# An eight-core decoder block: the order of the first transfers, and tile 0 scaled while the shift rows arrive

## The chip, the cores and the metric

The kernel runs on all 8 cores of one Trainium2 chip. Each core does one sequence of the batch and streams all the weights for itself; nothing is exchanged between cores. The metric is device time in microseconds (us) of the slowest core. An execution counts as slow, and is left out of every comparison, when one die is over 1% longer than the other at a lower granted TensorE clock, or when the run is over 1.5% above the fastest of the same kernel.

## The reference, cut to what matters

The block is a half-step SwiGLU feed-forward (FFN), a token mixer and a second FFN. Each is fed by an RMS norm whose scale and shift come from a conditioning vector:

```python
def ada_rmsnorm(x, g, shift, scale):
    return rmsnorm(x, g) * (1.0 + scale[:, None, :]) + shift[:, None, :]

def reference(x, c, w_mod, b_mod, g_ffn1, w_ffn1_in, w_ffn1_out, ...):
    c_act = jax.nn.silu(c)                                  # (8, 1024)
    mod = c_act @ w_mod[l] + b_mod[l]                       # (8, 9 * 1024)
    sh1, sc1, gt1, sh2, sc2, gt2, sh3, sc3, gt3 = jnp.split(mod, 9, axis=-1)
    h = ada_rmsnorm(x, g_ffn1[l], sh1, sc1)                 # x: (8, 4096, 1024) float32
    x = x + 0.5 * gt1[:, None, :] * swiglu_ffn(h, w_ffn1_in[l], w_ffn1_out[l])
    # ... mixer with sh2, sc2, gt2; second FFN with sh3, sc3, gt3; final norm
```

So nothing of the first FFN can be multiplied before 8 + 8 blocks of `w_mod` (those of `sc1` and `sh1`, 512 KB each) have been read. A core needs that much only once, at the very start.

Of the kernel before, what the change touches and what calls it, by code (L numbers as in the profile page):

```python
# [335 lines left out]
def build_program(n_tiles=SEQ // T, verbose=False):  # L336
# [17 lines left out]
    with es:  # L354
# [103 lines left out]

        def load_slab(nm, r, cast, prio=None, after=()):
            b = new(sl, f"{nm}{r}")  # L460
            if cast:
                src = dr(w_src[nm], r)
                dma("PL", lambda: b.ap, lambda: src, D_CAST, slot_sem(b, "PL"), [], [b], slab=True, prio=prio, after=after)
                d = scr[nm][r]
                dma("SP", lambda: d.ap, lambda: b.ap, D_SLAB, lambda: wb_sems[b.slot], [b], [d], prio=prio)
            else:
                d = scr[nm][r]
                dma("SP", lambda: b.ap, lambda: d.ap, D_SLAB, slot_sem(b), [d], [b], slab=True, prio=prio, after=after)
            return b
# [4 lines left out]
        dma("SP", lambda: crow.ap, lambda: crow_d[:, :], D_SLAB, lambda: sem_c, [], [crow], prio=-30)  # L474
        dma("PL", lambda: gates.ap, lambda: gates_d[:, :].rearrange("p (c n) -> p c n", c=8), 1.0, lambda: sem_g, [], [gates], prio=5000, after=(None,))
        sem_v, sem_c, sem_g = newsem("s_vecs"), newsem("s_crow"), newsem("s_gates")
# [11 lines left out]
        def mods(m, afters):  # L488

            for q in range(8):  # L490
                b = new(sl, f"mod{m + q}")
                src = dr(wmod_d, m + q)
                dma("SP", lambda b=b: b.ap.bitcast(F32), lambda s=src: s, D_SLAB, slot_sem(b), [], [b], slab=True,
                    prio=P.prio)
                o = modr[m].ap[:, q:q + 1]

                def f(b=b, o=o):
                    w = b.ap.bitcast(F32)
                    return lambda h: [h.scalar_tensor_tensor(out=w, in0=w, scalar=1.0, in1=crow.ap, op0=ALU.mult,  # L499
                                                             op1=ALU.mult, accum_out=o)]  # L500
                A("DVE", 1.3, f, [crow], [b, modr[m]], after=(afters[q],))
            tt(k_(modv[m].ap), k_(modr[m].ap), k_(V[:, V_BMOD + m:V_BMOD + m + 8]), ALU.add, [modr[m], vecs], [modv[m]], dur=0.17)

        def gs_op(m, g):
# [8 lines left out]
        P.prio = -20  # L513
        mods(M_SH1, [None] * 8)
        P.prio = 4000
# [42 lines left out]

        def ffn_in(slab, hbs, hids, j):

            w = lambda kc, o: (lambda: slab.ap[:, kc * 256 + o:kc * 256 + o + 128])
            ops = []
            for hb, hid in zip(hbs, hids):
                bg = new(ps, "g")
                mms(bg, [(w(kc, 0), lambda kc=kc, hb=hb: hb[kc].ap) for kc in range(8)], [slab] + hb)
                bu = new(ps, "u")
# [38 lines left out]
        for pi, tiles in enumerate(pairs):  # L605
            P.prio = 500 + pi * 100
            lp = -25 if pi == 0 else 400 + pi * 100
            xss = [load_x(x_dr, t, prio=(-22 if t == 0 else -15) if pi == 0 else lp, after=prev_in[8 * (t % 2):8 * (t % 2) + 8]) for t in tiles]
            hbs = [norm(xs, M_SC1, M_SH1, after=(last_in,), prio=300) for xs in xss]
            hids = [[] for _ in tiles]  # L610
            next_in = []
            for j in range(FC):
                slab = load_slab("w1i", j, pi == 0)
                ops = ffn_in(slab, hbs, hids, j)
                anchors.append((pi, ops[-1]))
# [19 lines left out]
        if len(pairs) == 1:  # L635
            mid = [mid[0]]

        psem = [VB(ap=None) for _ in range(8)]
# [179 lines left out]
        for s, op in seq:  # L818
            if op.nbytes == 0:
                for b in op.reads + op.writes:  # L820
                    if b.pool is sl and b not in use:
                        use[b] = len(use)
        loads.sort(key=lambda o: use[o.writes[0]])
        order = {o: k for k, o in enumerate(loads)}
# [142 lines left out]
```

## The kernel before: the parts that the change touches

A core's 4096 tokens are 8 tiles of 512. The first FFN takes the tiles in pairs: tiles 0 and 1, then 2 and 3, and so on. The weights are float32 in HBM, the chip's main memory. In the first pair each weight slab is loaded by a casting DMA to bf16 on GpSimd's queue and then written back as bf16 from SyncE's queue, so that later pairs can load it plainly.

The program is a list of operations. A planner simulates it once, picks by `prio` (low goes first) among those that are ready, and so fixes the order on each engine. Three kinds of relation matter here. A read or write of a buffer, and `sync`, become semaphore waits on the chip. `after` moves an operation only in the planned order; on the chip nothing waits for it. Every engine's list is written in the planned order, and ready work behind a wait was seen to stay behind it: in the changed kernel VectorE stood 4.3 us before two rows of `w_mod` while the scalings planned behind them were ready.

```python
def load_slab(nm, r, cast, prio=None, after=()):
    b = new(sl, f"{nm}{r}")                     # one of 10 slab buffers
    if cast:
        src = dr(w_src[nm], r)
        dma("PL", ..., D_CAST, slot_sem(b, "PL"), [], [b], slab=True, prio=prio, after=after)
        d = scr[nm][r]
        dma("SP", lambda: d.ap, lambda: b.ap, D_SLAB, lambda: wb_sems[b.slot], [b], [d], prio=prio)  # write-back
    else:
        dma("SP", ..., D_SLAB, slot_sem(b), [d], [b], slab=True, prio=prio, after=after)
    return b

def mods(m, afters):                            # one vector of `mod`: 8 rows of w_mod
    for q in range(8):
        b = new(sl, f"mod{m + q}")
        dma("SP", ..., D_SLAB, slot_sem(b), [], [b], slab=True, prio=P.prio)
        # VectorE: row * c_act, summed into modr[m][:, q]
        A("DVE", 1.3, f, [crow], [b, modr[m]], after=(afters[q],))
    tt(modv[m], modr[m], b_mod, ADD)            # all 8 sums, plus the bias

P.prio = -24
mods(M_SC1, [None] * 8)                         # scale rows
gs_op(M_SC1, V_G1)
P.prio = -20
mods(M_SH1, [None] * 8)                         # shift rows

def norm(xs, msc, msh, after=(), prio=None):
    r = stats(xs, after, prio)                  # 8 squares, 8 matmuls with ones, Ln, Exp
    for f in range(8):
        stt(t_, xs[f], gs[msc][f], r, MULT, MULT)        # VectorE: the scaling
        act(hb[f], t_, Identity, bias=modv[msh][f])      # ScalarE or VectorE: the shift

for pi, tiles in enumerate(pairs):
    lp = -25 if pi == 0 else 400 + pi * 100
    xss = [load_x(x_dr, t, prio=(-22 if t == 0 else -15) if pi == 0 else lp,
                  after=prev_in[8 * (t % 2):8 * (t % 2) + 8]) for t in tiles]
    hbs = [norm(xs, M_SC1, M_SH1, after=(last_in,), prio=300) for xs in xss]
    for j in range(FC):                         # 22 slabs of the first matrix
        slab = load_slab("w1i", j, pi == 0)
        ops = ffn_in(slab, hbs, hids, j)        # per tile: 8 gate and 8 up matmuls
        if j >= 3:
            next_in.append(ops[-1])
    prev_in = next_in
    if pi == 0:
        mods(M_GT1, [gt_anchor] * 8)            # gate rows
    for q in range(4):                          # 12 slabs of the second matrix
        slabs = [load_slab("w1o", 3 * q + s, pi == 0) for s in range(3)]
        ops = ffn_out(slabs, q, xss, hids, gth[M_GT1])
# ...
loads.sort(key=lambda o: use[o.writes[0]])      # slab buffers are given out in the order of first use
```

The norm of the next pair needs its x before the second matrix of this pair is done: in TensorE's order the eight statistics matmuls of tiles 2 and 3 stand within the work of the first pair.

## Time and profile before

| | before |
|---|---|
| time, median of 3 runs | 2489.81 us (2488.01 to 2493.35) |
| span of the profiled execution, slowest core | 2483.8 us |
| TensorE busy | 95% |
| first weight matmul | 65.82 us |
| TensorE reaches the statistics of tiles 2 and 3 | 220.50 us |
| TensorE goes on with weight matmuls | 235.36 us |

The page of the profile of before, its line of busy times and the chain of work that ended last (PE is TensorE, PEld its weight loads, DVE VectorE, ACT ScalarE, POOL GpSimd, SPq SyncE's issuing of transfers):

```profile
PE 2361.1 (95%) x11177; PEld 1114.5 (45%) x11392; DVE 1057.8 (43%) x1795; ACT 911.9 (37%) x1382; POOL 115.2 (5%) x221
...
PE 90%; DMA 5%; ACT 2%; issue 1%; SPq 1%; DVE 1%; POOL 0%; DVEq 0%; POOLq 0%; ACTq 0%
PE ps L443 90%; DMA sb_slab<-wmod 2%; DMA sb_c<-x 1%; SPq L450 1%; DMA sb_c<-xmid 1%; ACT sb_c L401 1%; DMA sb_slab<-w2o 1%; ACT sb_h L401 1%; DVE sb_c L419 0%; DVE sb_c L409 0%; DVE sb_slab L499 0%; DVE sb_ub L419 0%; ACT L401 0%; POOL y L450 0%; DVEq L113 0%
```

The kernel is bound by TensorE (PE). What the change can win is in the 5% that the chain spends on DMA: the rows of `wmod` and the tiles of x.

TensorE's timeline of before shows where that is. Columns: start, duration, engine, source line, operation, output and inputs, shapes, count, and in brackets the idle time before the group and what ended it. `sb_ones` are statistics, `sb_slab` are weight matmuls. Every matmul has one line of the program, so one goes by the inputs:

```profile
65.82 154.84 PE L443 MATMUL ps<-sb_h,sb_slab 128*128 128x512 bf16 x690 [15.81 <-ACT sb_h L401]
220.50 0.38 PE L443 MATMUL ps<-sb_h,sb_ones 128*128 128x512 bf16 x1
...
232.06 0.59 PE L443 MATMUL ps<-sb_h,sb_ones 128*128 128x512 bf16 x1 [5.14 <-ACT sb_h L401]
232.44 2.77 PE L443 MATMUL ps<-sb_h,sb_slab 128*128 128x512 bf16 x6
235.10 0.42 PE L443 MATMUL ps<-sb_h,sb_ones 128*128 128x512 bf16 x1
235.36 26.93 PE L443 MATMUL ps<-sb_h,sb_slab 128*128 128x512 bf16 x122
```

Three numbers will serve as marks: the **first weight matmul** (65.82), the **arrival** at the statistics of tiles 2 and 3 (220.50), and the **resume** of weight matmuls after them (235.36). The **stretch** between arrival and resume is 14.9 us here. At the next such change nothing is waited for and it takes 8.2 us (arrival 458.5, resume 466.73).

The same profile by windows. Columns: window, its length, busy time and count of PE, PEld, DVE, ACT and POOL, granted TensorE clock, mean busy share of the 16 DMA engines, GB/s:

```profile
12.00:28.00 16.00, 4.62 (x8) 0.84 (x8) 7.32 (x13) 7.62 (x11) 0.00 (x0) 1.00 0.99 325
34.00:46.00 12.00, 1.76 (x3) 0.31 (x3) 0.00 (x0) 1.92 (x4) 0.00 (x0) 1.00 1.02 199
72.00:86.00 14.00, 13.95 (x65) 6.37 (x65) 6.02 (x9) 3.61 (x6) 1.06 (x2) 1.00 0.38 119
86.00:100.00 14.00, 13.89 (x64) 6.37 (x65) 9.20 (x19) 2.39 (x4) 4.22 (x8) 1.00 0.88 149
```

DMA is full from 10 to about 70 us (a share of 0.97 to 1.02 by windows of 10 us), is then 38% busy for 14 us, and full again from 100 us (1.03 from 100 to 130 us). At 34 to 46 us it moves only 199 GB/s though it is full (1.02). The view of the DMA queues of that window says why: q0 carries the weight casts, q1 everything that SyncE issues.

```profile
q0 software_dynamic: 394, 1.43, 72.5%
q1 hardware_dynamic: 522, 0.95, 28.8%
```

The columns are packets, MB and share of the 16 engines. A cast packet holds an engine for 353 ns (72.5% of 12 us on 16 engines, over 394), a plain one for 106 ns; the cast packets are also larger here, 3.6 KB against 1.8 KB in the mean. So with both queues full in this window, plain loads got little more than a quarter of the time (28.8%).

### The profile page before, as it was taken

To read this page: it belongs to the slowest core of one execution; us is meant where nothing else is said; L and a number is where in the kernel's file an instruction comes from. 1 tells how busy PE (TensorE), PEld (TensorE's weight loads), DVE (VectorE), ACT (ScalarE), POOL (GpSimd) and SP (SyncE) were. 2 spreads that over 40 slices of the span, in tenths; PEclk is the share of its full clock that TensorE was granted. 3 is DMA by queue.
4 is the path that set the end of the run, shared out by engine and by line. 5 is a ranking of instruction groups with operands and counts; after the bars stand their busy time and mean duration, and the time that the engine had idled before them with its cause. 6 is when DMAs were issued, how large, how long until landed. Compare 5 with 4: busy or idle time off the path is not lost.

```text
span 2483.8 us, 34258 instructions; the slowest of 8 cores (2468.5 to 2483.8 us)
## 1 busy us (share of the span) xinstructions
PE 2361.1 (95%) x11177; PEld 1114.5 (45%) x11392; DVE 1057.8 (43%) x1795; ACT 911.9 (37%) x1382; POOL 115.2 (5%) x221
## 2 busy tenths in 40 slices
PE   1999999999999999899899999999999999999996
PEld 0444444444444444454354454454454454454442
DVE  3413133423342332785166175184274274373121
ACT  3213011301131120676157265265364364364122
POOL 0100100010001001000000000000000000000000
PEclk9999999999999999899999999999999999999998
DMA  9899489669856764554966555555555545555451
GB/s 274 192 217 230 160 213 221 165 189 220 221 166 181 188 189 164 163 166 159 200 207 203 186 179 178 187 178 179 187 178 178 187 170 187 187 170 186 153 188 66
DMA packets 131708, 460.31 MB, mean 185 GB/s; under 512 B 16048, under 2 KB 16176, under 8 KB 130864
## 3 DMA queue, kind: packets, MB, share of 16 engines
q1 hardware_dynamic: 113184, 378.15, 47.0%
q0 software_dynamic: 18352, 79.97, 16.0%
q8 instruction: 96, 1.57, 0.3%
q14 instruction: 76, 0.62, 0.1%
HBM read 446.78 MB, written 79.69 MB: 212 GB/s over the span
## 4 chain that ended last, share of the span: by engine, by line
PE 90%; DMA 5%; ACT 2%; issue 1%; SPq 1%; DVE 1%; POOL 0%; DVEq 0%; POOLq 0%; ACTq 0%
PE ps L443 90%; DMA sb_slab<-wmod 2%; DMA sb_c<-x 1%; SPq L450 1%; DMA sb_c<-xmid 1%; ACT sb_c L401 1%; DMA sb_slab<-w2o 1%; ACT sb_h L401 1%; DVE sb_c L419 0%; DVE sb_c L409 0%; DVE sb_slab L499 0%; DVE sb_ub L419 0%; ACT L401 0%; POOL y L450 0%; DVEq L113 0%
## 5 line engine op out<-in xcount | busy, mean ns | idle before, releaser
L443 PE MATMUL ps<-sb_h,sb_slab 128*128 128x512 bf16 x9776 | 2182.2, 380 | 28.7 <-ACT sb_h L401 15.8
L443 PEld LDWEIGHTS ps<-sb_h,sb_slab 128*128 128x128 bf16 x9984 | 977.7, 98 | 1196.1 <-issue 30.4
L423 DVE TENSOR_TENSOR sb_h<-ps,sb_c 128x512 bf16<-128x512 f32 x352 | 241.7, 691 | 784.0 <-PE ps L443 706.5
L401 ACT ACTIVATE sb_c<-ps 128x512 f32<-128x512 f32 x400 | 237.2, 596 | 882.0 <-PE ps L443 858.5
L401 ACT ACTIVATE sb_h<-sb_c 128x512 bf16<-128x512 f32 x241 | 148.9, 628 | 387.2 <-DVE sb_c L419 234.4
L419 DVE SCALAR_TENSOR_TENSOR sb_c<-ps,sb_gth,sb_c 128x512 f32<-128x512 f32 x128 | 95.2, 749 | 399.1 <-PE ps L443 390.6
L401 ACT ACT_TABLE_LOAD x102 | 130.9, 1283 | 211.5 <-PE ps L443 199.2
L419 DVE SCALAR_TENSOR_TENSOR sb_c<-sb_c,sb_gs 128x512 f32<-128x512 f32 x256 | 173.6, 745 | 39.9 <-ACT sb_c L401 39.9
L443 PE MATMUL ps<-sb_h,sb_ones 128*128 128x512 bf16 x313 | 106.6, 394 | 67.0 <-ACT sb_h L401 59.6
L499 DVE SCALAR_TENSOR_TENSOR sb_slab<-sb_slab,sb_crow 128x1024 f32<-128x1024 f32 x88 | 107.0, 1217 | 34.1 <-DMA sb_slab<-wmod 33.6
L443 PE MATMUL ps<-sb_ub,sb_slab 128*128 128x256 bf16 x1024 | 115.0, 273 | 4.3 <-DVE sb_c L409 3.3
L401 ACT ACTIVATE sb_h<-sb_c,sb_modv 128x512 bf16<-128x512 f32 x162 | 107.4, 719 | 15.6 <-DVE sb_modv L423 8.8
L443 PEld LDWEIGHTS ps<-sb_ub,sb_slab 128*128 128x128 bf16 x1024 | 99.5, 98 | 21.5 <-issue 8.1
L450 POOL DMA_DIRECT2D y<-sb_c x64 | 34.5, 540 | 1144.6 <-ACT sb_c L401 1104.7
L443 PEld LDWEIGHTS ps<-sb_h,sb_ones 128*128 128x128 bf16 x320 | 31.2, 98 | 118.5 <-issue 92.6
L419 DVE SCALAR_TENSOR_TENSOR sb_c<-ps,sb_modv,sb_c 128x512 f32<-128x512 f32 x64 | 48.0, 750 | 72.7 <-PE ps L443 72.5
L419 DVE SCALAR_TENSOR_TENSOR sb_c<-sb_ux,sb_vecs,sb_c 128x512 f32<-128x512 f32 x96 | 69.2, 743 | 1.3
L423 DVE TENSOR_TENSOR sb_c<-sb_c 128x512 f32<-128x512 f32 x96 | 61.6, 683 | 11.1 <-ACT sb_c L401 11.0
L419 DVE SCALAR_TENSOR_TENSOR sb_ub<-sb_c,ps 64x256 bf16<-64x256 f32 x128 | 53.8, 420 | 15.3 <-PE ps L443 11.8
L401 ACT ACTIVATE sb_c<-sb_c,sb_lam 128x512 f32<-128x512 f32 x64 | 49.1, 824 | 0.2
L450 POOL DMA_DIRECT2D xmid<-sb_c x64 | 34.8, 544 | 295.6 <-DVE sb_c L419 280.6
L401 ACT ACTIVATE sb_c<-sb_c 128x512 f32<-128x512 f32 x72 | 44.0, 626 | 2.2
(51 smaller groups left out, 532.8 us busy)
## 6 DMA issues: line engine op xcount, KB each, us to landing
sb_slab<-b_w2i SPq DMA_DIRECT2D x176, 512.0 KB, 3.8
sb_slab<-wmod SPq DMA_DIRECT2D x88, 512.0 KB, 6.1
sb_slab<-b_w2o SPq DMA_DIRECT2D x84, 512.0 KB, 3.7
sb_slab<-b_w1i SPq DMA_DIRECT2D x66, 512.0 KB, 6.0
sb_slab<-b_win SPq DMA_DIRECT2D x64, 512.0 KB, 4.0
sb_slab<-b_dcw SPq DMA_DIRECT2D x64, 512.0 KB, 3.6
sb_slab<-b_w1o SPq DMA_DIRECT2D x36, 512.0 KB, 5.5
sb_c<-x SPq DMA_DIRECT2D x64, 256.0 KB, 11.0
```

The source lines that it names most:

```text
L401: return A("ACT", dur, lambda: (lambda o, i: (lambda h: [h.activation(out=o, in_=i, func=func, bias=bias, scale=scale)]))(out(), in_()), r ...
L419: return A("DVE", dur, lambda: (lambda o, a, b: (lambda h: [h.scalar_tensor_tensor(out=o, in0=a, scalar=scalar, in1=b, op0=op0, op1=op1)]) ...
L423: return A("DVE", dur, lambda: (lambda o, a, b: (lambda h: [h.tensor_tensor(out=o, in0=a, in1=b, op=op)]))(out(), in0(), in1()), reads, wr ...
L443: return [h.matmul(o, lhsT=l, rhs=r, start=(first and i == 0), stop=(last and i == n - 1)) for i, (l, r) in enumerate(pr)]
L450: lambda: (lambda o, i: (lambda h: [h.dma_start(out=o, in_=i)]))(out(), in_()),
L499: return lambda h: [h.scalar_tensor_tensor(out=w, in0=w, scalar=1.0, in1=crow.ap, op0=ALU.mult, op1=ALU.mult, accum_out=o)]
```

## The change

The intent: the first transfers go in the order in which they are needed. Scale rows, x of tile 0, shift rows, then x of tile 1 and the third and later weight casts. Tile 0 is scaled while the shift rows are still arriving, and the first slab's gate matmuls for each block of the norm may start when that block is ready.

Its parts: (A) slab buffers are given out by priority before order of use, so that the 16 rows go ahead of weight casts; (B) x of tile 1 is planned after the last shift row; (C) casts from the third slab on wait at run time for the last shift row's multiplication, and are planned after x of tile 1; (D) the norm of tile 0 gets a high priority; (E) the first slab's gate matmuls are split into eight operations that wait separately; (F) the load of the mixer's gate weights moves to a later point.

```diff
-        def load_slab(nm, r, cast, prio=None, after=()):
+        def load_slab(nm, r, cast, prio=None, after=(), sync=()):
 ...
-                dma("PL", ..., D_CAST, slot_sem(b, "PL"), [], [b], slab=True, prio=prio, after=after)
+                dma("PL", ..., D_CAST, slot_sem(b, "PL"), [], [b], slab=True, prio=prio, after=after, sync=sync)
 ...
-        dma("PL", lambda: gates.ap, ..., [], [gates], prio=5000, after=(None,))
 ...
-        mods(M_SH1, [None] * 8)
+        sh1_last = mods(M_SH1, [None] * 8)
 ...
+                if split:
+                    for kc in range(8):
+                        mms(bg, [(w(kc, 0), ...hb[kc].ap)], [slab, hb[kc]], first=(kc == 0), last=(kc == 7))
+                else:
+                    mms(bg, [... for kc in range(8)], [slab] + hb)
 ...
-            xss = [load_x(x_dr, t, prio=(-22 if t == 0 else -15) if pi == 0 else lp, after=prev_in[8 * (t % 2):8 * (t % 2) + 8]) for t in tiles]
-            hbs = [norm(xs, M_SC1, M_SH1, after=(last_in,), prio=300) for xs in xss]
+            if pi == 0:
+                xss = [load_x(x_dr, t, prio=-22 if t == 0 else -15, after=[None if t == 0 else sh1_last] * 8) for t in tiles]
+                hbs = [norm(xs, M_SC1, M_SH1, prio=-23 if t == 0 else 300) for t, xs in zip(tiles, xss)]
+            else:
+                (as before)
 ...
-                slab = load_slab("w1i", j, pi == 0)
-                ops = ffn_in(slab, hbs, hids, j)
+                slab = load_slab("w1i", j, pi == 0, sync=(sh1_last,) if pi == 0 and j >= 2 else (),
+                                 after=[xb.lw for xb in xss[-1]] if pi == 0 and j >= 2 else ())
+                ops = ffn_in(slab, hbs, hids, j, split=(j == 0))
 ...
+        dma("PL", lambda: gates.ap, ..., [], [gates], prio=5000, sync=(mid[0],))
 ...
-        loads.sort(key=lambda o: use[o.writes[0]])
+        loads.sort(key=lambda o: (min(o.prio, 0), use[o.writes[0]]))
```

More of the change, by code (lines that the diff above doesn't have):

```diff
@@ L462, in load_slab @@
                 src = dr(w_src[nm], r)
-                dma("PL", lambda: b.ap, lambda: src, D_CAST, slot_sem(b, "PL"), [], [b], slab=True, prio=prio, after=after)
+                dma("PL", lambda: b.ap, lambda: src, D_CAST, slot_sem(b, "PL"), [], [b], slab=True, prio=prio, after=after, sync=sync)
                 d = scr[nm][r]
@@ L474, in build_program @@
         dma("SP", lambda: crow.ap, lambda: crow_d[:, :], D_SLAB, lambda: sem_c, [], [crow], prio=-30)
-        dma("PL", lambda: gates.ap, lambda: gates_d[:, :].rearrange("p (c n) -> p c n", c=8), 1.0, lambda: sem_g, [], [gates], prio=5000, after=(None,))
         sem_v, sem_c, sem_g = newsem("s_vecs"), newsem("s_crow"), newsem("s_gates")
@@ L500, in f @@
                                                              op1=ALU.mult, accum_out=o)]
-                A("DVE", 1.3, f, [crow], [b, modr[m]], after=(afters[q],))
+                last = A("DVE", 1.3, f, [crow], [b, modr[m]], after=(afters[q],))
             tt(k_(modv[m].ap), k_(modr[m].ap), k_(V[:, V_BMOD + m:V_BMOD + m + 8]), ALU.add, [modr[m], vecs], [modv[m]], dur=0.17)
+            return last
         def gs_op(m, g):
@@ L557, in norm, with ffn_in @@
             return hb
-        def ffn_in(slab, hbs, hids, j):
+        def ffn_in(slab, hbs, hids, j, split=False):
             w = lambda kc, o: (lambda: slab.ap[:, kc * 256 + o:kc * 256 + o + 128])
@@ L564, in ffn_in @@
                 bg = new(ps, "g")
-                mms(bg, [(w(kc, 0), lambda kc=kc, hb=hb: hb[kc].ap) for kc in range(8)], [slab] + hb)
+                if split:
+                    for kc in range(8):
+                        mms(bg, [(w(kc, 0), lambda kc=kc, hb=hb: hb[kc].ap)], [slab, hb[kc]], first=(kc == 0), last=(kc == 7))
+                else:
+                    mms(bg, [(w(kc, 0), lambda kc=kc, hb=hb: hb[kc].ap) for kc in range(8)], [slab] + hb)
                 bu = new(ps, "u")
@@ L607, in build_program @@
             lp = -25 if pi == 0 else 400 + pi * 100
-            xss = [load_x(x_dr, t, prio=(-22 if t == 0 else -15) if pi == 0 else lp, after=prev_in[8 * (t % 2):8 * (t % 2) + 8]) for t in tiles]
-            hbs = [norm(xs, M_SC1, M_SH1, after=(last_in,), prio=300) for xs in xss]
+            if pi == 0:
+                xss = [load_x(x_dr, t, prio=-22 if t == 0 else -15, after=[None if t == 0 else sh1_last] * 8) for t in tiles]
+                hbs = [norm(xs, M_SC1, M_SH1, prio=-23 if t == 0 else 300) for t, xs in zip(tiles, xss)]
+            else:
+                xss = [load_x(x_dr, t, prio=lp, after=prev_in[8 * (t % 2):8 * (t % 2) + 8]) for t in tiles]
+                hbs = [norm(xs, M_SC1, M_SH1, after=(last_in,), prio=300) for xs in xss]
             hids = [[] for _ in tiles]
@@ L636, in build_program @@
             mid = [mid[0]]
+        dma("PL", lambda: gates.ap, lambda: gates_d[:, :].rearrange("p (c n) -> p c n", c=8), 1.0, lambda: sem_g, [], [gates], prio=5000, sync=(mid[0],))
         psem = [VB(ap=None) for _ in range(8)]
```

## The prediction

> **What bounds the kernel now.** TensorE. Busy 95% of the 2483.8 us span; the chain of waits is 90% matmul. The change touches only the start and what follows from it. Timeline: real matmuls start at 65.82 us. In those 65 us the limit is DMA (share 0.97 to 1.02 per 10 us window from 10 to 70). The chain there is mostly scale/shift row loads (pieces of 14.9 and 23.3 us); the last of 16 rows is multiplied at 58-59 us, although tile 1 of x (landed 32 to 48 us) and three weight casts went ahead of them. A second cost falls at the change to tiles 2 and 3: the last x tiles land at 231 and 234 us, and the statistics stretch from 220.5 to 235.4 us takes 14.9 us against 8.2 us at the next such change (458.5 to 466.7). Between 72 and 86 us the DMA share is only about 37%, from 86 to 96 about 83%: some 10 us unused.
>
> **What changes.** Only the first stage's order differs; no work is removed. Ahead of the first weight matmul go vectors, 16 rows, x tile 0 (11.1 MB) and two casts; x tile 1, the third cast, six gate rows and the gate weights move behind. Estimate: 11.1 MB at the 325 GB/s of 12-28 us is 34 us, two casts at 3.2 us (23% of 42 us for three), a slow first 10 us: rows landed about 45-46 us, first weight matmul about 48.5 us (17 us earlier).
>
> Not all is won. TensorE is in order, and after 14 weight matmuls stand the statistics of tile 1. Its x queues behind the shift rows and one write-back. When the last shift row is multiplied, eight casts are released at once. [...]from 34 to 46 us, beside casts, the hardware queue moved 522 packets, 0.95 MB (79 GB/s) against 394 cast packets taking 72.5% of the time. I estimate four x tiles through before the casts bite, the other four at 79 GB/s: last x of tile 1 at 60-64 us, then about 5.6 us (square, statistics, table load 1.28, Ln, Exp, scale, shift). So 48 weight matmuls are done at about 77.5 us against 79.1 before: only 1 to 3 us won here.
>
> The rest comes later: eight casts in flight fill the idle DMA of 72-96 us, so next x should land about 222-226 us and most of the 8 us lost at 220-235 goes.
>
> **Prediction.** 2482 us (8 less), range 2473 to 2491. Faster by over 2% 0.01, same 0.98, slower 0.01.
>
> **What would show it.** First weight matmul 46-51 us; then TensorE idle for over 8 us waiting on squares of tile 1; x of tile 1 landing at intervals of 3 us or more once casts start; DMA share above 0.8 through 70-96 us; statistics stretch of tiles 2 and 3 down from 14.9 us to 8-11 us.
>
> **What would make it wrong.** If x of tile 1 slips past the casts (landed by 53 us), the start wins 10 us or more, and the gain is 12-18 us. If casts starve it to beyond 70 us, the start loses and the total is level. If SyncE blocks on its in-order waits (a gate row waits until TensorE has finished weight slab 4), next x comes no earlier and the switch gives nothing back.

The 79 GB/s and the 72.5% are measured (before, 34 to 46 us). The sum is as it stands: 34 us for 11.1 MB, 6.4 us for two casts and the slow first 10 us (a DMA share of 0.71, 163 GB/s in before) give rows at 45 to 46 us; of the 17 us won at the first weight matmul 1 to 3 us are kept, and with the stretch 4 to 7 us shorter (8 to 11 instead of 14.9) that makes the 8 us of the total. The 5.6 us after the last x are an estimate: in before a square takes 0.63 us, a statistics matmul 0.59, the table load 1.28, Ln 0.69, Exp 0.63, a scaling 0.75 and a shift 0.67, together 5.2 us without the hand-overs. That TensorE takes its list in order is seen in after: it stood 6.02 and 2.96 us before two statistics (at 222.17 and 226.14 us) and ran the six weight matmuls that stand behind them only at 226.52 us.

## The result

Beside three rounds of the changed kernel, the fast runs of the kernel before took 2488.01, 2489.81 and 2493.35 us; a fourth, 2537.59 us, is over 1.5% above the fastest, so it counts as slow and is left out. The changed kernel's fast runs took 2479.28, 2480.40 and 2479.32 us; two more runs, 2631.43 and 2702.04 us, were slow ones (die 1 at a clock of 0.93 and 0.90) and are left out. The ratio of after to before is 0.9957, 95% interval 0.9934 to 0.998: 10.7 us less, "same" by the 2% mark. A later repetition on another chip gave 0.9953 (0.9938 to 0.9967), 11.8 us less. A ratio is the mean time of one kernel's fast runs over that of the other's of the same rounds, so it is not quite the ratio of the medians quoted.

So the total came inside the predicted range, a little below its middle (2482). The steps on the way to it did not come as predicted, and that is the subject of the rest.

The page of after, the same lines (the chain by engine, which reads 90% PE and 5% DMA again, is left out):

```profile
PE 2370.5 (96%) x11392; PEld 1114.2 (45%) x11392; DVE 1062.3 (43%) x1803; ACT 908.2 (37%) x1376; POOL 115.3 (5%) x221
...
PE ps L443 90%; DMA sb_c<-x 1%; ACT sb_c L401 1%; DMA sb_slab<-w1o 1%; DMA sb_c<-xmid 1%; DMA sb_slab<-wmod 1%; SPq L450 1%; DMA sb_slab<-w2o 1%; DVE sb_c L419 0%; ACT sb_h L401 0%; DVE sb_c L409 0%; ACT L401 0%; DVE sb_slab L498 0%; DVE sb_ub L419 0%; POOL y L450 0%
```

(The counts of PE differ because some matmul records are missing from the trace of before: 11177 matmuls beside 11392 weight loads.) In the chain, `wmod` has gone from 2% to 1%, and the cast of `w1o`, a slab of the second matrix of the first pair, has come in with 1%.

TensorE's timeline of after:

```profile
53.55 4.60 PE L443 MATMUL ps<-sb_h,sb_slab 128*128 128x512 bf16 x14 [23.97 <-ACT sb_h L401]
...
68.36 141.75 PE L443 MATMUL ps<-sb_h,sb_slab 128*128 128x512 bf16 x656 [1.15 <-ACT sb_h L401]
209.94 0.38 PE L443 MATMUL ps<-sb_h,sb_ones 128*128 128x512 bf16 x1
...
222.17 1.01 PE L443 MATMUL ps<-sb_h,sb_ones 128*128 128x512 bf16 x2 [6.02 <-DVE sb_h L413]
226.14 0.59 PE L443 MATMUL ps<-sb_h,sb_ones 128*128 128x512 bf16 x1 [2.96 <-ACT sb_h L401]
226.52 2.77 PE L443 MATMUL ps<-sb_h,sb_slab 128*128 128x512 bf16 x6
229.08 0.63 PE L443 MATMUL ps<-sb_h,sb_ones 128*128 128x512 bf16 x1
229.51 32.83 PE L443 MATMUL ps<-sb_h,sb_slab 128*128 128x512 bf16 x149
```

The first weight matmul comes 12.3 us earlier, the arrival 10.6 us earlier, the resume only 5.9 us earlier. The start won ten microseconds and the change to tiles 2 and 3 gave almost half of them back. All eight cores show it:

| mark, us | before, core 6 | after, core 7 | before, mean of 8 cores | after, mean of 8 cores |
|---|---|---|---|---|
| first weight matmul | 65.8 | 53.5 | 65.8 | 53.0 |
| arrival | 220.5 | 209.9 | 220.1 | 209.8 |
| resume | 235.4 | 229.5 | 231.9 | 226.0 |
| stretch (resume less arrival) | 14.9 | 19.6 | 11.8 | 16.2 |
| rest of the span after the resume | 2248.4 | 2248.2 | 2246.6 | 2245.9 |

Here core 6 and core 7 are the slowest cores of the two profiled executions. The rest after the resume is level within 1 us, so the first 235 us are where the difference lies. What sets the resume is when the last x of tile 3 lands: at 227.14 us on core 7, after which its square starts at 227.22 us and weight matmuls resume at 229.51.

VectorE's timeline of after explains the first mark. Line 498 is the multiplication of a row of `w_mod`, line 419 on `sb_c` the scaling of tile 0:

```profile
33.65 1.23 DVE L498 SCALAR_TENSOR_TENSOR sb_slab<-sb_slab,sb_crow 128x1024 f32<-128x1024 f32 x1 [10.08 <-DMA sb_slab<-wmod]
37.94 1.23 DVE L498 SCALAR_TENSOR_TENSOR sb_slab<-sb_slab,sb_crow 128x1024 f32<-128x1024 f32 x1 [3.05 <-DMA sb_slab<-wmod]
39.09 5.38 DVE L419 SCALAR_TENSOR_TENSOR sb_c<-sb_c,sb_gs 128x512 f32<-128x512 f32 x8
44.39 1.22 DVE L498 SCALAR_TENSOR_TENSOR sb_slab<-sb_slab,sb_crow 128x1024 f32<-128x1024 f32 x1
...
52.42 0.17 DVE L423 TENSOR_TENSOR sb_modv<-sb_modr,sb_vecs 128x8 f32<-128x8 f32 x1
55.37 2.02 DVE L413 TENSOR_TENSOR sb_h<-sb_c 128x512 bf16<-128x512 f32 x3 [0.47 <-DMA sb_c<-x]
```

The planner put two shift rows ahead of the eight scalings. The scalings were ready at 32.4 us, when ScalarE had done the Exp of tile 0's statistics. VectorE stood waiting for a row then (the last 1.2 of 10.08 us), multiplied it, waited another 3.05 us for the second, and began the 5.38 us of scaling only at 39.09, by when other rows had landed. From 44.39 on it multiplies six rows back to back at 1.34 us apiece, with no wait among them: at that point it is VectorE, not DMA, that the first weight matmul waits for. In the two waits VectorE was idle for 4.3 us with the scalings ready behind the rows in its list. The last line is a square of tile 1: it waited only 0.47 us for its x.

The windows of after:

```profile
34.00:46.00 12.00, 0.00 (x0) 0.00 (x0) 8.84 (x15) 0.00 (x0) 0.00 (x0) 1.00 1.00 315
46.00:53.00 7.00, 0.00 (x0) 0.00 (x0) 6.37 (x12) 0.32 (x1) 0.15 (x1) 1.00 0.95 287
53.00:66.00 13.00, 12.46 (x52) 5.40 (x53) 5.28 (x10) 8.77 (x14) 4.29 (x8) 1.00 0.97 167
72.00:86.00 14.00, 14.00 (x66) 6.37 (x65) 4.10 (x7) 4.37 (x9) 1.59 (x3) 1.00 1.03 225
86.00:100.00 14.00, 14.00 (x66) 6.34 (x65) 2.99 (x5) 2.27 (x4) 0.53 (x1) 1.00 1.03 216
```

From 34 to 53 us no cast competes but the tail of the second one (landed at 37.6 us), so DMA moves 315 and 287 GB/s where before had 199 from 34 to 46 us. GpSimd issues eight casts from 52.85 us on, and the rate falls to 167. Between 72 and 100 us DMA is now full instead of 38% and 88% busy. But x of tile 1 is through before the casts fill DMA. The plain queue, from 53 to 57 us and then from 57 to 66 us:

```profile
q1 hardware_dynamic: 274, 0.72, 46.5%
q1 hardware_dynamic: 6, 0.02, 0.6%
```

In the first 4 us it still moves 180 GB/s, not the 79 GB/s that I had predicted for x of tile 1. The first packet of a released cast starts at 55.10 us, the last x of tile 1 has landed at 56.6 us (54.8 to 56.6 us on the eight cores), and the first of these casts lands at 61.15 us. After 57 us the plain queue gets next to nothing, but by then only write-backs of weight slabs stand in it.

### The profile page after: what moved, and what is told of

Its sections match the earlier page's. It is cut to its first block, busy times and chain, and to the rows that moved or that the text cites. A ratio compares the mean times of both kernels' runs of the same rounds, so it can differ in the third digit from the quotient of the medians.

```text
span 2477.7 us, 34471 instructions; the slowest of 8 cores (2466.4 to 2477.7 us)
## 1 busy us (share of the span) xinstructions
PE 2370.5 (96%) x11392; PEld 1114.2 (45%) x11392; DVE 1062.3 (43%) x1803; ACT 908.2 (37%) x1376; POOL 115.3 (5%) x221
## 3 DMA queue, kind: packets, MB, share of 16 engines
q8 instruction: 96, 1.57, 0.3%
## 4 chain that ended last, share of the span: by engine, by line
PE 90%; DMA 5%; ACT 2%; issue 1%; DVE 1%; SPq 1%; POOL 0%; DVEq 0%; POOLq 0%; ACTq 0%
PE ps L443 90%; DMA sb_c<-x 1%; ACT sb_c L401 1%; DMA sb_slab<-w1o 1%; DMA sb_c<-xmid 1%; DMA sb_slab<-wmod 1%; SPq L450 1%; DMA sb_slab<-w2o 1%; DVE sb_c L419 0%; ACT sb_h L401 0%; DVE sb_c L409 0%; ACT L401 0%; DVE sb_slab L498 0%; DVE sb_ub L419 0%; POOL y L450 0%
```

## The experiments

Twelve runs. Each gave the reference's result. Marks are given as means over the 8 cores of the profiled execution, and where a group of TensorE is quoted, it is of the slowest core. Three groups of runs ran on three chips, each beside its own runs of the kernel before, so totals are compared within a group.

| run | chip | fast runs, mean us | ratio to before (95%) | first | arrival | resume |
|---|---|---|---|---|---|---|
| before, first trace | | | | 65.8 | 220.1 | 231.9 |
| before again | 14 | 2489.7 | none | 67.3 | 221.4 | 233.7 |
| after, first trace | | 2479.7 | 0.9957 (0.9934 to 0.998) | 53.0 | 209.8 | 226.0 |
| after again | 1 | 2478.2 | 0.9953 (0.9938 to 0.9967) | 53.6 | 210.7 | 224.8 |
| casts free | 0 | 2484.8 | 0.9968 (0.9887 to 1.0048) | 58.7 | 223.2 | 231.4 |
| scale first | 0 | 2476.4 | 0.9934 (0.9854 to 1.0014) | 50.5 | 211.9 | 222.3 |
| next x earlier | 0 | 2479.9 | 0.9948 (0.9844 to 1.0052) | 51.6 | 218.9 | 227.1 |
| before, next x earlier | 0 | 2491.9 | 1.0019 (0.9806 to 1.0232) | 65.4 | 219.5 | 227.7 |
| w1o casts late | 1 | 2472.6 | 0.993 (0.9915 to 0.9945) | 53.1 | 210.2 | 218.4 |
| both | 1 | 2475.4 | 0.9941 (0.9925 to 0.9958) | 51.7 | 213.1 | 221.3 |
| order alone | 1 | 2484.3 | 0.9972 (0.9955 to 0.9989) | 64.9 | 218.8 | 230.4 |
| x of tile 1 free | 14 | 2480.8 | 0.996 (0.9943 to 0.9978) | 57.8 | 211.9 | 225.7 |
| no split | 14 | 2480.4 | 0.9959 (0.9938 to 0.998) | 54.2 | 211.7 | 225.8 |
| casts after x1 | 14 | 2475.5 | 0.9939 (0.9921 to 0.9957) | 51.4 | 213.9 | 222.1 |

Mean of the kernel before in the same rounds: 2491.1 us on chip 0 (with one run of 2511.48 that counts as fast, against 2483.5 to 2485.8 of the others, and makes the intervals of that group wide; without it the mean would be 2484.3), 2490.0 on chip 1, 2490.7 on chip 14.

My theory after reading the two traces: the start won ten microseconds because the casts were released late and x of tile 1 had the queue to itself; the loss at tiles 2 and 3 came because DMA, now full from 53 us on, still carried things needed later (casts of the second matrix and their write-backs) ahead of or beside the next x. Rivals: the casts' late release is no part of the gain (the order of rows is); or TensorE simply arrives before the next x was ever planned to be loaded.

### Casts free (e1_casts_free)

Part C is undone: casts may start as soon as they have a buffer.

```diff
-  slab = load_slab("w1i", j, pi == 0, sync=(sh1_last,) if pi == 0 and j >= 2 else (), after=[...])
+  slab = load_slab("w1i", j, pi == 0)
```

> The changed kernel, but weight casts from the third on no longer wait for the last shift row (a buffer still has to be free). Theory A (holding the casts back is what lets the shift rows and x of tile 1 through): casts enter as the first shift rows are consumed, from about 35 us, the last shift rows and x of tile 1 come at the 79 GB/s seen beside casts, the first weight matmul is at 58 us or later (53.6 in the changed kernel) and x of tile 1 lands after 70 us. The planner also lets 88 weight matmuls of tile 0 go first here, so TensorE need not stop for tile 1. Theory B (the order of the first 16 rows alone does it): first weight matmul within 1 us of 53.6, and the run within 2 us of the changed kernel.

The first weight matmul comes at 58.7 us in the mean, 5.7 us later than in after, and the arrival at 223.2, which is 13.4 us later and even later than in before. x of tile 1 lands only from 65.6 to 79.7 us on the slowest core. TensorE has a gap of 3.41 us before 102 us, in which it waits for the norm of tile 1. DMA is 5% busy from 90 to 100 us and 37% from 100 to 120 us on the slowest core, as it was idle in before: GpSimd issues no cast from 60 to 110 us, and its next one waits for TensorE. The stretch at tiles 2 and 3 is 8.2 us on all cores, so the resume (231.4) is that of before. Taking part C out loses the start and leaves DMA idle later. It does not test the wait purely, since without C the planner also puts 88 weight matmuls of tile 0 ahead of the statistics of tile 1. The total is unclear by its interval, and level with before (2484.3) if the odd run is left out.

### Scale first (e2_scale_first)

All eight shift rows' multiplications are planned after the last scaling of tile 0.

```diff
-        sh1_last = mods(M_SH1, [None] * 8)
+        n_ops = len(P.ops)
+        sh1_last = mods(M_SH1, [None] * 8)
+        sh1_rows = [o for o in P.ops[n_ops:] if o.eng == "DVE"][:8]
 ...
+                scales = [o for o in P.ops[n_ops:] if o.eng == "DVE"][:8]
+                for o in sh1_rows:
+                    o.after.append(scales[-1])
```

> The changed kernel, with the eight scalings of x of tile 0 placed on VectorE ahead of all eight shift rows, instead of after the second. Theory A (VectorE's fixed order, not DMA, set the first weight matmul: from 39.1 to 52.4 us it works without a pause on rows that had already landed, because it waited until 37.9 us for the second shift row): first weight matmul at 48 to 50 us instead of 53.6. But the casts are then released 4 to 5 us earlier, while x of tile 1 is still in the queue behind two write-backs; beside casts it moves at about 79 GB/s, so TensorE stops after 14 weight matmuls and the start as a whole is no better, or some 5 us worse, than in the changed kernel. Theory B (no starving): the 5 us stay won up to the change to tiles 2 and 3.

On the slowest core VectorE now scales from 33.23 to 38.6 us, multiplies eight rows without a wait and has the shift vector at 49.24 us, against 52.42. The first weight matmul comes at 50.5 us in the mean, 2.5 us earlier. The arrival is not earlier (211.9 against 209.8): the casts are released earlier too, and x of tile 1 then shares the queue with them; VectorE waits 2.48, 0.30 and 1.56 us for pieces of it. So VectorE's order did cost about 2.5 us of the first mark (3.2 us between the slowest cores), and by itself this is not worth anything at the second. The eight cores show the starving: on the four whose casts were released at 47.8 to 49.3 us TensorE waited 5 to 9 us in all at the statistics of tile 1, on the other four, released at 49.6 us or later, at most 1.4 us. The third mark is nevertheless 2.5 to 3.7 us earlier than in the two traces of after, and the total some 2 to 3 us lower than theirs. No run of after stood beside this one on its chip, and what brings the resume forward was not looked into.

### Next x earlier (e5_nextx)

The loads of tiles 2 and 3 are planned at earlier weight slabs of the first pair.

```diff
-  after=prev_in[8 * (t % 2):8 * (t % 2) + 8]
+  after=[prev_in[(8 * (t % 2) + f) // 2] for f in range(8)]
```

> The changed kernel, with x of tiles 2 and 3 placed in the load queue twice as early (two tiles of x per weight slab, from slab 3 to slab 10 instead of slab 3 to slab 18). Theory A (at the change to tiles 2 and 3 the changed kernel waits only for the last x tiles, which stand too late in a full queue): the statistics stretch falls from 19.6 us to 8 to 9 us, x of tile 3 has landed before 205 us, the time falls about 11 us below the changed kernel, to 2469 us. Theory B (total DMA work before that point is the limit): the wait moves to weight casts, TensorE gets gaps between 100 and 260 us instead, and the time stays within 3 us of the changed kernel.

The stretch at tiles 2 and 3 is 8.2 us on every core: next x is in time. But the resume is 227.1, no better than after's 226.0. TensorE waits earlier instead, mostly at one place (5.0 to 9.0 us on the eight cores). VectorE's line just before it comes first here, then TensorE's (line 498 is the multiplication of a row of `w_mod`):

```profile
158.78 1.22 DVE L498 SCALAR_TENSOR_TENSOR sb_slab<-sb_slab,sb_crow 128x1024 f32<-128x1024 f32 x1 [10.06 <-DMA sb_slab<-wmod]
161.40 58.59 PE L443 MATMUL ps<-sb_h,sb_slab 128*128 128x512 bf16 x259 [8.92 <-DVE sb_h L423]
```

The trace says how the wait came there. SyncE issues all sixteen pieces of the next x from 92 to 131 us, among the gate rows, while DMA is full throughout (share 1.02 to 1.03 from 86 to 165 us). The last gate row, issued at 127.57 us, lands only at 158.6 us. VectorE stands 10.06 us before it; behind it in VectorE's order come four products of the feed-forward (line 423, from 160.56 us), and TensorE goes on when the first of them is done. The casts are delayed too: in after GpSimd issues the last eight of the first matrix from 129.84 to 142.4 us, here the same eight from 126.23 to 161.7 us, most of them released by a row's multiplication. But they are not what TensorE waited for: the next slab that it took up had landed at 137.3 us. With DMA full, an earlier place in the order only moved the wait from one transfer to another. The rival that the next x was merely planned too late falls, for after.

### Before, next x earlier (e6_before_nextx)

The same edit on the kernel before.

> The kernel before with the same earlier place for x of tiles 2 and 3, and nothing else. Theory A: first weight matmul unchanged at 65.8 us, statistics stretch from 14.9 us down to 8 to 9 us, the time 6 to 7 us less than before, so about 2483 us. Theory B (total DMA work is the limit): no gain.

Here it does remove the wait: the stretch is 8.2 us on every core and the resume 227.7, about 4 us earlier than in before. Before had idle DMA from 72 to 100 us, which an earlier load could use. The total stays unclear: two runs at 2480.39 and 2482.15 us, and one of 2513.11 us at a clock of 0.978 that counts as fast. I draw the conclusion from the trace only.

### After again (e4_after_again)

The changed kernel, unaltered, on the chip of the next three runs.

> The changed kernel itself, on the same chip and rounds as the next three, so that they can be compared with it. Its traced core resumed weight matmuls after the statistics of tiles 2 and 3 at 229.5 us; expected 228 to 231 us, and a time of 2478 to 2481 us.

It repeats: 2476.26 to 2480.14 us, first mark 53.6, arrival 210.7, resume 224.8. The slowest core resumes at 226.9 us, a little earlier than expected.

### Casts of the second matrix late (e9_w1o_late)

After, with the casts of the second matrix from its fourth slab on held back until the last x of tile 3 has landed. The first three slabs, needed first, are not held.

```diff
+                if pi == 0:
+                    w1o_casts += [b.lw for b in slabs]
 ...
+            if pi == 1:
+                gate = xss[-1][-1].lw           # the load of the last x of tile 3
+                for o in w1o_casts[3:]:
+                    o.sync.append(gate)
+                    o.deps.add(gate)
```

> The changed kernel, but the casts of the first FFN's output weights from the fourth slab on wait until the last x of tile 3 has landed (they are needed only after it). Six or seven casts at about 3.3 us and as many write-backs at about 1.6 us of DMA leave the stretch before 230 us. Theory A (up to the change to tiles 2 and 3 the DMA is full, and x of tiles 2 and 3 shares it with work that is needed later): start as in the changed kernel, the statistics stretch falls from 19.6 us to 8 to 10 us, weight matmuls resume at 217 to 220 us, time 9 to 11 us below the changed kernel if the late casts keep up with the output matmuls. Theory B (x of tiles 2 and 3 is held by something else, such as buffers freed late by TensorE): the stretch stays above 15 us and the time is within 3 us of the changed kernel.

The 3.3 and 1.6 us are estimates: in before three casts took 23.0% of the 42 us from 20 to 62 us, 3.2 us each, and 512 KB at 325 GB/s (before, 12 to 28 us) take 1.6 us.

TensorE's timeline of this kernel:

```profile
212.48 0.38 PE L443 MATMUL ps<-sb_h,sb_ones 128*128 128x512 bf16 x1
...
219.17 1.46 PE L443 MATMUL ps<-sb_h,sb_slab 128*128 128x512 bf16 x6
220.46 0.38 PE L443 MATMUL ps<-sb_h,sb_ones 128*128 128x512 bf16 x1
220.68 41.39 PE L443 MATMUL ps<-sb_h,sb_slab 128*128 128x512 bf16 x188
```

There is no bracket left: no wait, a stretch of 8.2 us on all eight cores. The first two marks are those of after (53.1 and 210.2), and the resume is 218.4 in the mean against 224.8 of after on the same chip, 6.4 us earlier. 5.6 us of it are in the total: 2472.6 against 2478.2 us, with runs of 2470.75 to 2474.48 against 2476.26 to 2480.14. That is less than the 9 to 11 us that I had expected; after the resume the cores take 1.8 us longer in the mean (2247.1 against 2245.3). It is the best version, 17.4 us under before. So what held the next x back in after was work for the same DMA that nobody needed yet.

SyncE's own queue shows one way in which it did so. In the timeline of SyncE of after, the last x and what follows it:

```profile
195.36 3.82 SPq L450 DMA_DIRECT2D sb_c<-x  x1
199.27 23.43 SPq L450 DMA_DIRECT2D b_w1o<-sb_slab  x6
```

and in that of this kernel:

```profile
183.51 3.67 SPq L450 DMA_DIRECT2D sb_c<-x  x2
206.99 19.55 SPq L450 DMA_DIRECT2D b_w1o<-sb_slab  x5
```

In the program a write-back (`b_w1o<-sb_slab`) waits until its cast has landed; from 135 to 199 us of after SyncE stood 15.5 us in four such waits for casts of the second matrix. Write-backs of the second matrix stand between the loads of x there, two of these loads go 0.15 and 0.16 us behind one (188.79 and 195.36 us), and the last x is issued at 195.4 to 199.2 us; here it is issued by 187.2 us, 12 us earlier. The second way is the landing itself: the last loads of x took a median of 34.1 us from issue to landing in after (two loads, issued from 188.8 us), and 15.7 us here (four loads, issued from 178.3 us). The edit acts on both, and I have no run that parts them.

### Both (e10_both)

The edits of "scale first" and of "casts of the second matrix late" together.

> The last kernel together with the earlier scaling of tile 0 on VectorE. Alone that scaling let the first weight matmul start 3 us earlier, of which under 2 us were left at the second tile's statistics and nothing at 210 us, because small gaps took it back while DMA was full. Theory A (with DMA relieved, what the start wins is kept): 1 to 3 us below the last kernel, first weight matmul near 50 us. Theory B: equal to the last kernel within 1 us.

It is not faster than the latter alone, as I had expected (2475.4 against 2472.6); that it is slower isn't shown, since its runs of 2472.39 to 2477.35 overlap the other's of 2470.75 to 2474.48. The stretch is 8.2 us, but the arrival is 213.1 instead of 210.2. On the slowest core:

```profile
61.03 0.38 PE L443 MATMUL ps<-sb_h,sb_ones 128*128 128x512 bf16 x1 [1.44 <-DVE sb_h L413]
64.80 0.59 PE L443 MATMUL ps<-sb_h,sb_ones 128*128 128x512 bf16 x1 [3.39 <-DVE sb_h L413]
68.78 0.58 PE L443 MATMUL ps<-sb_h,sb_ones 128*128 128x512 bf16 x1 [3.39 <-ACT sb_h L401]
```

These are statistics of tile 1, whose x lands about 4 us apart. The casts were issued from 49.03 us here, against 52.85 in after. This is the starving that I had predicted for after, and on this core at the size that I had predicted, 8.2 us in all: it needs the casts only some 4 us earlier. Over the eight cores the waits add up to between 0 and 8.5 us, the longest on the two cores whose casts were released first (49.0 and 49.5 us), and none on the core where they were released last (55.7 us).

### Order alone (e8_order_only)

The kernel before with part A only.

```diff
-        loads.sort(key=lambda o: use[o.writes[0]])
+        loads.sort(key=lambda o: (min(o.prio, 0), use[o.writes[0]]))
```

> The kernel before with one line of the change: the order of loads follows negative priorities first, so the eight scale rows go ahead of x of tile 0 and of the shift rows. x of tile 1 still goes ahead of the last six shift rows and casts are not held back. Theory A (all parts of the order of need are wanted): scale rows done near 22 us, but the last shift row only at 55 us or later, first weight matmul 58 to 64 us (before 65.8, changed 53.6), weight matmuls resume after the statistics of tiles 2 and 3 at 230 to 236 us. Theory B (the row order is the whole effect): first weight matmul within 2 us of 53.6.

The first weight matmul stays at 64.9 us. The rival that the order of rows is the gain falls for the first mark: without B to D the same transfers still compete before the first matmul. For the total it does not fall. That is 5.7 us under before, with an interval clear of 1, so about half of the 11.8 us of the whole change on the same chip. The trace can't say where these lie: it was taken in the slowest of the four executions (2487.87 us, the others 2482.64 to 2483.51), and its resume is 230.4 against 231.9 and 233.7 in the two traces of before. What part A is worth, and by what way, stays open.

### Before again (e12_before_again)

> The kernel before itself, for a second trace of it. Its first trace came from a run of 2485.3 us, while most timed runs of it took 2488 to 2493 us, so the pair of traces shows only 6 of the 11 us that the times show. Theory A (the rest is in the same place, because the last x of tiles 2 and 3 lands at a different time in each run and core): in a slower run the statistics stretch of the slowest core is longer than 14.9 us and the rest after it is within 2 us of the first trace. Theory B: the start or the rest after 235 us differs instead.

The totals differ by 10.7 to 11.8 us while the first two traces show only 5.9 us at the resume. The first trace of before was taken in an execution of 2485.3 us, which is one of its quick ones. In this second trace the slowest core resumes at 238.25 us after a stretch of 17.6 us, and the rest of its span is 2249.5 us, against 2248.4 in the first trace. The mean resume is 233.7, so 8.9 us later than that of "after again". The gain thus lies before the resume in this pair too, and varies between executions by a few microseconds: stretches of single cores lie between 8.2 and 17.6 us within this one execution.

### x of tile 1 free (e7_x1_free)

Part B is undone: x of tile 1 may be planned before the shift rows.

```diff
-  after=[None if t == 0 else sh1_last] * 8
+  after=[None] * 8
```

> The changed kernel, but x of tile 1 no longer has to follow the last shift row in the load queue; the planner then puts it after the second shift row, and spreads the scaling of tile 1 among the shift rows on VectorE. Theory A (x of tile 1 ahead of the shift rows costs its own 2.1 MB, 6 to 7 us at 325 GB/s): last shift row and first weight matmul 5 to 10 us later than in the changed kernel, at 59 to 64 us, but then no stop for tile 1. Theory B (the same bytes are needed anyway before TensorE can run on without a stop): weight matmuls then run without a gap and reach the statistics of tiles 2 and 3 within 3 us of the changed kernel's 210 us.

The first weight matmul is 4.8 us later than in after (57.8), but the arrival only 2.1 us (211.9) and the resume level (225.7). TensorE runs 704 weight matmuls from 57.69 without a gap, because tile 1 is ready. The first mark by itself is thus no measure of the gain.

### No split (e3_nosplit)

Part E is undone.

```diff
-  ops = ffn_in(slab, hbs, hids, j, split=(j == 0))
+  ops = ffn_in(slab, hbs, hids, j, split=False)
```

> The changed kernel without the finer waits in the first accumulation (the first eight weight matmuls wait for all eight normalized tiles, as before). All eight follow within 3 us of each other, so: first weight matmul 1.5 to 2.5 us later (55 to 56 us), arrival at the statistics of tiles 2 and 3 at most 2 us later, and the time within 2 us of the changed kernel, because x of tiles 2 and 3 limits there.

First mark 54.2 (after: 53.0 and 53.6), arrival 211.7 (209.8 and 210.7), resume 225.8 (226.0 and 224.8). The split is worth about 1 us at the first marks and nothing that can be measured at the end.

### Casts after x of tile 1 (e13_casts_after_x1)

"Both", with the third and later casts held until x of tile 1 has landed instead of until the last shift row is multiplied.

```diff
-  sync=(sh1_last,) if pi == 0 and j >= 2 else ()
+  sync=[xb.lw for xb in xss[-1]] if pi == 0 and j >= 2 else ()
```

> The version with late output-weight casts and with tile 0 scaled ahead of the shift rows, but the third and later casts now wait until x of tile 1 has landed, not for the last shift row. In the version without this, TensorE stood still three times for 1.4, 3.4 and 3.4 us while x of tile 1 came 4 us apart beside the casts. Theory A (casts starved x of tile 1): those three pauses go, first weight matmul near 50 us, weight matmuls resume after the statistics of tiles 2 and 3 at 213 to 217 us, and the time is 2 to 5 us below the version with late casts alone (0.9930 of before), about 0.991. Theory B (x of tile 1 is late for another reason): the pauses stay.

The pauses for x of tile 1 are gone, but on most cores TensorE now waits 1.9 to 6.1 us for the third weight slab, whose cast starts too late. Arrival 213.9, resume 222.1, total 2475.5 us: level with "both", and no better than holding back the second matrix alone (ratio 0.9939 against 0.993, on different chips), where I had expected 0.991. The third slab was needed too soon to be held back.

Not tried by themselves: part D, the priority of tile 0's norm, and part F, the gate weights' later load. What they are worth stays open.

## Why the prediction was right or wrong

**The total was right: 2482 predicted, 2479.3 (median of the fast runs) measured, in the range 2473 to 2491.** It was right as a sum although two of its terms were wrong, because both are held together by one quantity that I had estimated well: when the last x of tiles 2 and 3 lands. I predicted 222 to 226 us; in after it lands at 227.1 us on the slowest core and at 223.9 us in the mean of eight (220.9 to 227.7), against 234.3 and 230.4 in before. TensorE resumes then, whenever it arrived, so the arrival, 8 us earlier than predicted, and the longer stretch had to cancel. That the total came so close is partly luck: the resume was predicted 8 us earlier and came 5.9 us earlier in the first traces, 8.9 us in the second pair, while the totals differ by 10.7 to 11.8 us.

| term | predicted, us | measured, slowest cores of the first traces | measured, mean of 8 cores |
|---|---|---|---|
| first weight matmul | 17 earlier | 12.3 earlier | 12.8 earlier |
| arrival at tiles 2 and 3 | 1 to 3 earlier | 10.6 earlier | 10.3 earlier |
| stretch there | 4 to 7 shorter | 4.7 longer | 4.4 longer |
| resume | 8 earlier | 5.9 earlier | 5.9 earlier |

**First weight matmul at about 48.5 us (46 to 51): wrong by 5 us.** Measured 53.55. The landing of the rows came some 2 us late: 45 to 46 us predicted, 47.9 us on this core (46.9 to 48.3 us on the eight). What I left out was VectorE's work behind it: two rows before the scalings, with waits, then 5.38 us of scaling, then six rows at 1.34 us apiece. "Scale first" gets 50.4 us on its slowest core and so shows this as the cause of some 3 of the 5 us.

**"only 1 to 3 us won here": this is the step that failed.** Measured 10.3 to 10.6 us at the arrival, where I had let the starving of tile 1 eat all but 1 to 3. In the terms of the sum: four pieces of x of tile 1 were to pass before the casts bite, the other four were to crawl at 79 GB/s until 60 to 64 us, TensorE was to stop after 14 weight matmuls, and 48 of them were to be done at 77.5 us. All eight pieces passed, the last at 56.6 us; TensorE waited 1.15 us, and 48 weight matmuls were done at 67.2 us (67.4 in the mean of eight cores, 78.7 in before). The mechanism was real and the time was wrong. I had the casts released by the multiplication of the last row, which is what happens, but took this to follow the landing at once; VectorE's order put the release at 52.85 us, about 5 us after the landing. In between x of tile 1 had DMA nearly for itself (287 GB/s from 46 to 53 us), and the first packet of these casts started only at 55.10 us. "Both" shows the starving when the release is at 49.03 us, with pauses of 3.39 us; "casts free" shows the start lost with no hold at all. My own clause "If x of tile 1 slips past the casts (landed by 53 us), the start wins 10 us or more" is nearly what happened (the last piece landed at 56.6 us, and the start won 10); its second half, a gain of 12 to 18 us, did not follow.

**"statistics stretch of tiles 2 and 3 down from 14.9 us to 8-11 us": wrong in sign.** Measured 19.6 us on the slowest core (16.3 in the repetition). I had fixed the arrival near that of before and let x come earlier. TensorE came 10.6 us earlier, x some 7 us (its last piece landed at 234 us in before), and the difference was waited out. Of the 19.57 us, 8.2 are the work itself, 8.98 are the two waits in brackets, and the remaining 2.4 are matmuls at a lower clock after the waits: the six weight matmuls at 226.52 take 2.77 us, the same six in the kernel with late casts 1.46 us, at a granted clock of 1.00 (218 to 221 us). After the waits of 6.02 and 2.96 us the granted clock was 0.50 in the window of after from 226 to 230 us:

```profile
226.00:230.00 4.00, 3.86 (x10) 1.45 (x11) 1.22 (x2) 2.75 (x4) 0.00 (x0) 0.50 0.76 308
```

**"If SyncE blocks on its in-order waits": not in the form that I feared.** SyncE issued the last x at 199.2 us in after against 210.8 us in before. Standing behind the write-backs (four waits, 15.5 us) may have cost time all the same: the kernel with late casts issues the last x 12 us earlier still, but no run parts this from the landing.

**DMA share above 0.8 from 70 to 96 us: right.** 1.03 was measured from 72 to 100 us. As predicted, it fills with casts, and with their write-backs. The two queues share the 16 engines here: with next to nothing else in them, SyncE's queue took 99.4% of their time (before, 12 to 28 us) and GpSimd's 100.7% (after, 57 to 66 us). In after from 72 to 86 us GpSimd's casts took 72.6% of their time and SyncE's transfers 29.6%, together all of it. "Next x earlier" shows what this means within one queue: next x, moved forward among SyncE's transfers, delayed the last gate row, until TensorE stood for 8.92 us. Across the queues, holding nine casts of the second matrix back brought the resume 6.4 us forward. Whether the casts' share of the DMA or their write-backs' place in SyncE's queue costs more was not separated; the edit delays both.

**That the total is nearer 11 us than the 5.9 us between the first two traces** is explained in part: the second trace of before resumes later, and its difference from "after again" is 8.9 us in the mean. The rest, some 2 us, is within what single executions of one kernel differ by.

## What to carry to other kernels

An early start is banked only at the next place where the same resource is full: follow the gain to the next wait and name what will end that. Where DMA was full here (a share of 1.02 to 1.03 in "next x earlier"), moving a transfer forward moved the wait to another one (8.92 us); what helped was to hold back, with a real wait and not only a place in the order, a transfer that is needed later still (the resume 6.4 us earlier). And when a release hangs on an operation rather than on a landing, read when that operation runs, since a few microseconds decided here whether tile 1 was starved.

## What else the traces show of the hardware

- A packet of a casting DMA held an engine longer than a plain one: 353 ns against 106 ns (34 to 46 us of before). Part of that goes with size (3.6 KB against 1.8 KB), but not all: in after from 72 to 86 us each queue moved 430 packets of the same size, 1.57 MB each, and the casts took 72.6% of the time, the plain ones 29.6%, which is 378 ns against 154 ns a packet. So with both queues full, the time was not shared by halves.
- With casts in the queue a core moved 167 to 225 GB/s at a DMA share of 0.97 to 1.03 (after, 53 to 66 and 72 to 100 us), without any 287 GB/s at 0.95 (after, 46 to 53 us) and 325 GB/s at 0.99 (before, 12 to 28 us).
- The granted clock in the records does not show every slow stretch. From 65.80 to 70.00 us of before it reads 1.00, while ten matmuls begin after 15.81 us of idle time in 4.18 us, 0.42 us each, against 1.46 us for six in the kernel with late casts, 0.24 us each. Why these ten are slower was not shown.
- With TensorE 95% busy, the cores of the fast runs have a mean granted clock of 0.978 to 0.993. In the two slow runs of after (2631 and 2702 us) the slower die was at 0.93 and 0.90, and the lowest core of all runs was at 0.816 (a slow run of "both", 2943 us). What lowers the clock in the slow runs was not looked into.
